# First modulation of a two-layer diffusion backbone: four steps of two K chunks instead of five steps

## The chip, the cores and the metric

One core of a Trainium2 chip runs the whole program. The metric is the device time of one execution in microseconds (us), lower is better. In the profile the engines are PE (TensorE matmul), PEld (TensorE weight load), DVE (VectorE), ACT (ScalarE), POOL (GpSimd) and SP (SyncE, which here issues every DMA; SPq is its queue). L12 stands for line 12 of the kernel.

## The reference, cut to what matters

Two layers (DEPTH 2) of width D = 1024 work on 256 latent tokens `x` and 256 context tokens `ctx`. Each layer is a half-step gated FFN, a mixer (neighbourhood attention in layer 0, a short convolution in layer 1) and another half-step FFN. Only the very start matters here:

```
m  = (silu(c)     @ ada_w[0] + ada_b[0])   # 9 vectors of 1024, latent tokens
mc = (silu(c_ctx) @ ada_w[0] + ada_b[0])   # the same for the context tokens
h  = x   * (1 + m[1])  + m[0]              # first modulation
hc = ctx * (1 + mc[1]) + mc[0]
a, u = split(h @ ffn_w_in[0, 0], 2);  g = silu(a) * u     # first FFN (and the same for hc)
```

All is float32. Products of matrices are made from two reduced-precision parts: every operand is split into `hi` (rounded) and `lo` (the rest), and each product is hi*hi + lo*hi + hi*lo, three matmuls.

## The kernel before

**Tiling.** The K dimension of 1024 is cut into eight chunks of 128 (`KC = 8`). The first FFN keeps its output transposed: one matmul of `f0_mm` (L537 hi*hi, L538 lo*hi, L539 hi*lo) has 128 columns of the weight as the stationary side and all 512 tokens, latent and context, as the moving side, into one PSUM bank of 128x512. Six banks are open at once (`b0`, `b1`), so that a K chunk serves six groups `g` of three matmuls, eighteen matmuls in all; the eight chunks make 144.

**The start in steps.** Before the first FFN can use a K chunk, its modulation has to be there. `start_step(k0, n)` makes it for n chunks beginning at k0: it loads the columns of two modulation vectors from `ada_w` (L478, tiles `ar`), the bias `ada_b` (L481, tile `ab`, once for four chunks) and the columns of x and ctx (L485, tiles `x` and `xc`, for two chunks at a time); it multiplies silu(c) and silu(c_ctx) with the `ada_w` tiles on PE (L490, result `ada`), adds the bias (L495, `rows`), turns x into columns (L500, `xT`), turns the rows into per-partition columns (L522, `mc`; L524 and L525, `mcol`), and calls `mod`. Of these, `mod` reads the transposed x from PSUM twice: ACT makes `hi` (`h0h`, L509, scale and bias as per-partition operands, rounded on writing), then DVE makes the unrounded value (`h`, L513) and `lo` = value minus hi (`h0l`, L515). The steps are (0,1), (1,1), (2,2), (4,2), (6,2): two of one chunk and three of two. A generator yields between the parts, and the loop over `steps` puts them between the groups of `f0_mm` of the step before; the tables `NA` and `NB` say how many parts go ahead of each group.

**Weights.** `w1(p, [u])` loads a pair of weight blocks for panel p and K chunks 2u and 2u+1 (two DMAs of 256 KB, L175, tile `w1r`), and splits them: ACT makes `w1h` in two halves (L178), DVE `w1l` in two halves (L181).

**Order.** PE runs in the order of the program text (`manual_schedule`). The instructions of ACT, DVE and of SP's DMA queue are ordered by a list scheduler at build time: by priority, which is the order of the text, moved ahead by `tc.high_priority(offset=...)`, and by when the scheduler thinks that the inputs are ready; the order is then fixed, and every engine runs its list strictly in order. In the start, `w_early[0]` is 0 (no offset for the weights' split), and `mod` has the offset `W_EARLY` = 40. Tiles come from pools with few buffers: `ar` tiles from two pools of together five free buffers, raw weights from four (`WB`), the PSUM banks of `ada`, `xT` and `mc` from two (`PB["tp"]`).

Of the kernel before, what the change touches and what calls it, by code (L numbers as in the profile page):

```python
# [32 lines left out]
W_EARLY = 40  # L33
# [1 line left out]
LN_EARLY = 60  # L35
LEAD = 5
TAIL = 3
XAT = 1
A_LAG = 2
A_PRE = 2  # L40
NX_AT = 2
# [13 lines left out]
V_EARLY = 70  # L55
W_HI = 2
W_LO = 2
NA = (1, 2, 1, 0, 0, 0)
NB = (2, 2, 1, 0, 0, 0)
E0 = (0,)  # L60
E2 = (0, 5, 7)

# [2 lines left out]
def backbone_kernel(  # L65
# [6 lines left out]
    nc = tc.nc  # L72
    sync = nc.sync
# [7 lines left out]
    hp = phase.__enter__()  # L81

    uid = [0]
    w_early = [0]
# [16 lines left out]
    def tpb(s="tp"):  # L101
        return bank("tp", s)
# [59 lines left out]
    def wunit(srcs, kn, s):  # L162

        raw = wp.tile([P, UN], F32, tag="wr", bufs=WB[0], name=nm(s + "r"))
        ext[1] += 1
        if ext[0] and ext[1] % (5 + ext[0]) in (E0 if ext[0] == 1 else E2):
            hi = hp.tile([P, UN], F32R, tag="whx", bufs=ext[0], name=nm(s + "h"))
            lo = hp.tile([P, UN], F32R, tag="wlx", bufs=ext[0], name=nm(s + "l"))
        else:
            hi = wp.tile([P, UN], F32R, tag="wh", bufs=WB[1], name=nm(s + "h"))  # L170
            lo = wp.tile([P, UN], F32R, tag="wl", bufs=WB[2], name=nm(s + "l"))
        rv, hv, lv = (t[:, :kn * 512].rearrange("p (a b) -> p a b", a=kn) for t in (raw, hi, lo))
        with tc.high_priority(offset=w_early[0]):
            for src, c in srcs:
                sync.dma_start(rv[:, :, c:c + src.shape[2]], src)  # L175
            m = kn * 512
            for a in range(0, m, m // W_HI):
                nc.scalar.activation(hi[:, a:a + m // W_HI], raw[:, a:a + m // W_HI], AF.Copy)  # L178
            for a in range(0, m, m // W_LO):
                b = a + m // W_LO  # L180
                nc.vector.tensor_tensor(out=lo[:, a:b], in0=raw[:, a:b], in1=hi[:, a:b].bitcast(F32), op=ALU.subtract)  # L181
        return hv, lv
# [5 lines left out]
    def wpair(w, u, c0, c1, s):  # L188
        if c1 == c0 + 256:
# [26 lines left out]
                            in1=idv[:, 1, :, 0:2], op=ALU.add)  # L216
# [234 lines left out]
    xt = []  # L451
# [6 lines left out]
    mcol = cp.tile([P, KC, 2, 2], F32, tag="mcol", name="mcol")  # L458
# [4 lines left out]
    def start_tile():  # L463
        nar[0] += 1
        if nar[0] % 5 in (2, 4):
            return hp.tile([P, 2, 512], F32, tag="pt", bufs=4, name=nm("ar")).rearrange("p a b -> p (a b)")
        return hp.tile([P, D], F32, tag="ar", bufs=3, name=nm("ar"))

    def start_step(k0, n):

        ps = tpb("ada")
        m = n * P
        kt = 512 // m
        last = KC // kt - 1
        for a in range(KC // kt):
            w = start_tile().rearrange("p (k m c) -> p k m c", k=kt, m=2)
            for i in range(2):
                sync.dma_start(w[:, :, i], bass.AP(ada_w.tensor, ada_w.offset + a * kt * P * 9 * D + i * D + k0 * P,  # L478
                                                   [[9 * D, P], [P * 9 * D, kt], [1, m]]))
            if a == last and k0 % 4 == 0:  # L480
                sync.dma_start(ab0[k0 // 4][0:64], bass.AP(ada_b.tensor, ada_b.offset + k0 * P, [[D, 2], [0, 32], [1, 512]]))  # L481
            if a == (last if k0 else XAT) and k0 % 2 == 0:
                for t in range(4):
                    src = x[0] if t < 2 else ctxt[0]
                    sync.dma_start(xt[t][k0 // 4][:, k0 % 4 * P:k0 % 4 * P + 256],  # L485
                                   src[(t % 2) * P:(t % 2 + 1) * P, k0 * P:k0 * P + 256])
            for i in range(kt):
                for j in range(2):
                    o = 64 * (i % 2) + 32 * j
                    nc.tensor.matmul(ps[o:o + 32, 0:m], cst[:, a * kt + i, :], w[:, i, j, :],  # L490
                                     start=(a == 0 and i < 2), stop=(a == last and i >= kt - 2))
            if (a + 1) % (n if n == 1 else 2) == 0:
                yield
        rows = sp.tile([P, 256], F32, tag="s2", bufs=S2, name=nm("rows"))
        nc.vector.tensor_tensor(out=rows[:, 0:m], in0=ps[:, 0:m], in1=ab0[k0 // 4][:, k0 % 4 * P:k0 % 4 * P + m], op=ALU.add)  # L495

        def xT(k):
            px = tpb("xT")
            for t in range(4):
                nc.tensor.transpose(px[:, t * P:(t + 1) * P], xt[t][k // 4][:, (k % 4) * P:(k % 4 + 1) * P], ident)  # L500
            return px

        def mod(k, px):
            t = sp.tile([P, 512], F32, tag="s2", bufs=S2, name=nm("h"))
            hi, lo = act(F32R, "h0h"), act(F32R, "h0l")
            with tc.high_priority(offset=W_EARLY):
                for v in range(2):
                    s = slice(v * 256, (v + 1) * 256)
                    nc.scalar.activation(hi[:, s], px[:, s], AF.Identity, bias=mcol[:, k, 0, v:v + 1],  # L509
                                         scale=mcol[:, k, 1, v:v + 1])  # L510
                for v in range(2):
                    s = slice(v * 256, (v + 1) * 256)
                    nc.vector.tensor_scalar(t[:, s], px[:, s], mcol[:, k, 1, v:v + 1], mcol[:, k, 0, v:v + 1],  # L513
                                            op0=ALU.mult, op1=ALU.add)
                nc.vector.tensor_tensor(out=lo, in0=t, in1=hi.bitcast(F32), op=ALU.subtract)  # L515
            hT0.append((hi, lo))

        px = xT(k0)
        yield
        pc = tpb("mc")  # L520
        for i in range(n):
            nc.tensor.matmul(pc[:, 4 * i:4 * i + 4], rows[:, i * P:(i + 1) * P], sel, start=True, stop=True)  # L522
        pv = pc[:, 0:4 * n].rearrange("p (k m v) -> p k m v", k=n, m=2)
        nc.vector.tensor_copy(mcol[:, k0:k0 + n, 0, :], pv[:, :, 0, :])  # L524
        nc.vector.tensor_scalar(mcol[:, k0:k0 + n, 1, :], pv[:, :, 1, :], 1.0, None, op0=ALU.add)  # L525
        mod(k0, px)
        yield
        if n > 1:
            mod(k0 + 1, xT(k0 + 1))
            yield  # L530

    def f0_mm(ps, units, j, z, ks):
        s = slice(z * 256 + j * P, z * 256 + (j + 1) * P)
        for k in ks:
            hi, lo = units[k // UK]
            lh, ll = hi[:, k % UK, s], lo[:, k % UK, s]
            nc.tensor.matmul(ps, lh, hT0[k][0], start=(k == 0), stop=False)  # L537
            nc.tensor.matmul(ps, ll, hT0[k][0], start=False, stop=False)  # L538
            nc.tensor.matmul(ps, lh, hT0[k][1], start=False, stop=(k == KC - 1))  # L539
# [31 lines left out]
    w_early[0] = W_EARLY  # L571
# [315 lines left out]
    steps = [(h + i, qt) for h in range(0, NH, 2) for qt in range(2) for i in range(2)]  # L887
# [10 lines left out]
    for i in range(len(steps) + LAG + V_LAG):  # L898
# [13 lines left out]
        n = int(credit)  # L912
# [10 lines left out]
        j = i - LAG - V_LAG  # L923
# [77 lines left out]
    g, hTs, later = sub_end(sc_w_out[0], lhs_T(yT), KC, 1, 1, 5, 1.0, (1, 6), "wo", order_late(KU))  # L1001
# [56 lines left out]
```

## Time and profile before

| | us |
|---|---|
| median of three runs | 1295.72 |
| the three runs | 1291.27, 1295.72, 1295.99 |
| the profiled execution, as a whole | 1290.21 |
| its span, first to last instruction | 1288.4 |
| PE busy in the span | 1256.5 (98%) |
| DVE busy | 954.7 (74%) |
| ACT busy | 591.0 (46%) |
| instructions | 17192 |

The profile is one execution taken by the hardware profiler. A row of a timeline begins with the start in the span and a duration, then the engine, the line, the operation, output and inputs, and in brackets how long the engine was idle before and what it was waiting for. A row of the grouped view has the shapes, the count, and after the bar the summed busy time in us and the mean in ns. The busy time of a matmul is modelled and reaches over the start of the next one, so the distance between two starts says more than the duration.

### The profile page before, as it was taken

The page shows a single profiled execution, that of the slowest core. Times are in us where ns is not written, and L with a number is a line of the kernel's source. Part 1 is how long each engine was busy: PE and PEld are TensorE (multiplying, and loading weights), DVE is VectorE, ACT ScalarE, POOL GpSimd, SP SyncE. Part 2 cuts the span into 40 slices and gives each one's busy share as a digit, 9 for nine tenths or more (in the row PEclk, how much of TensorE's full clock was granted, in tenths as well). Part 3 has the DMA queues.
Part 4 walks back from the last instruction along what each step waited for, and adds up shares of the span by engine and source line. Part 5 has one row for each costly group of instructions (what it writes and reads, how often), then busy time and mean ns, then how long its engine had stood idle before and what let it go on. Part 6 is the DMA issues. An engine that isn't in the chain of part 4 may idle for free.

```text
span 1288.4 us, 17192 instructions
## 1 busy us (share of the span) xinstructions
PE 1256.5 (98%) x5890; PEld 1005.4 (78%) x5890; DVE 954.7 (74%) x1683; ACT 591.0 (46%) x1148; POOL 40.4 (3%) x69
## 2 busy tenths in 40 slices
PE   7999999999999999988999999999999999999997
PEld 4787778788778877766787787887788877788886
DVE  3599877595658767788997888867878688855545
ACT  2433132412326456677554535645435645655431
POOL 0000000000001111120000000000000000000000
PEclk9999999999999999989999999999999999999999
DMA  9978668484622744464998988677887764676641
GB/s 285 284 238 260 187 187 289 153 299 150 216 66 85 217 90 90 92 149 130 314 333 267 325 315 298 205 220 222 290 298 244 211 218 147 214 213 187 226 158 50
DMA packets 204018, 271.26 MB, mean 211 GB/s; under 512 B 30028, under 2 KB 149300, under 8 KB 203930
## 3 DMA queue, kind: packets, MB, share of 16 engines
q1 hardware_dynamic: 203930, 270.16, 66.9%
q8 instruction: 46, 0.75, 0.2%
q14 instruction: 42, 0.34, 0.1%
HBM read 267.93 MB, written 2.17 MB: 210 GB/s over the span
## 4 chain that ended last, share of the span: by engine, by line
PE 81%; DVE 7%; DMA 6%; ACT 3%; issue 1%; SPq 1%; POOL 0%; DVEq 0%; ACTq 0%
PE w L156 15%; PE w L157 14%; PE w L159 14%; PE f L537 6%; PE f L539 6%; PE f L538 6%; DMA w1r<-in_ffn_w_in_dram 4%; DVE w1l L181 2%; PE wkv L156 2%; PE wkv L159 2%; PE wkv L157 2%; PE wc L156 2%; PE wc L157 2%; PE wc L159 2%; DMA ar<-in_ada_w_dram 1%
## 5 line engine op out<-in xcount | busy, mean ns | idle before, releaser
L178 ACT ACTIVATE w1h<-w1r 128x512 fp32r<-128x512 f32 x352 | 203.1, 626 | 185.7 <-PE w L159 71.4
L181 DVE TENSOR_TENSOR w1l<-w1r,w1h 128x512 fp32r<-128x512 f32 x352 | 227.6, 685 | 66.7 <-ACT w1h L178 63.5
L156 PE MATMUL w<-w1h,hTh 128*128 128x512 f32 x528 | 210.8, 399 | 3.3 <-ACT hTh L105 3.3
L243 DVE SCALAR_TENSOR_TENSOR acc<-ar,cst,acc 128x512 f32<-128x512 f32 x266 | 187.5, 746 | 33.6 <-DMA ar<-in_ada_w_dram 33.3
L157 PE MATMUL w<-w1l,hTh 128*128 128x512 f32 x528 | 207.0, 392 | 0.0
L156 PE MATMUL w<-w2h,gh 128*128 128x512 f32 (+1 forms) x446 | 175.4, 394 | 0.0
L157 PE MATMUL w<-w2l,gh 128*128 128x512 f32 (+1 forms) x446 | 173.4, 389 | 0.0
L178 ACT ACTIVATE w2h<-w2r 128x512 fp32r<-128x512 f32 x176 | 101.5, 624 | 140.9 <-PE w L159 122.2
L159 PE MATMUL w<-w1h,hTl 128*128 128x512 f32 x528 | 163.4, 391 | 0.7 <-DVE hTl L106 0.7
L181 DVE TENSOR_TENSOR w2l<-w2r,w2h 128x512 fp32r<-128x512 f32 x176 | 114.0, 686 | 42.1 <-ACT w2h L178 41.4
L537 PE MATMUL f<-h0h,w1h 128*128 128x512 f32 x352 | 139.3, 396 | 0.0
L539 PE MATMUL f<-h0l,w1h 128*128 128x512 f32 x352 | 137.8, 392 | 0.0
L538 PE MATMUL f<-h0h,w1l 128*128 128x512 f32 x352 | 137.8, 391 | 0.0
L159 PE MATMUL w<-w2h,gl 128*128 128x512 f32 (+1 forms) x446 | 136.3, 387 | 0.0
L156 PEld LDWEIGHTS w<-w1h,hTh 128*128 128x128 f32 x528 | 99.2, 188 | 27.2 <-ACT hTh L105 4.6
L159 PEld LDWEIGHTS w<-w1h,hTl 128*128 128x128 f32 x528 | 98.9, 188 | 23.9 <-DVE hTl L106 1.5
L157 PEld LDWEIGHTS w<-w1l,hTh 128*128 128x128 f32 x528 | 99.2, 188 | 20.3 <-DVE w1l L181 0.3
L156 PEld LDWEIGHTS w<-w2h,gh 128*128 128x128 f32 x446 | 83.7, 188 | 21.8 <-issue 1.7
L159 PEld LDWEIGHTS w<-w2h,gl 128*128 128x128 f32 x446 | 83.3, 188 | 18.8
L157 PEld LDWEIGHTS w<-w2l,gh 128*128 128x128 f32 x446 | 83.7, 188 | 17.4
L537 PEld LDWEIGHTS f<-h0h,w1h 128*128 128x128 f32 x352 | 66.2, 188 | 17.9 <-issue 4.1
L539 PEld LDWEIGHTS f<-h0l,w1h 128*128 128x128 f32 x352 | 66.2, 188 | 14.4
(176 smaller groups left out, 1703.1 us busy)
## 6 DMA issues: line engine op xcount, KB each, us to landing
w1r<-in_ffn_w_in_dram SPq DMA_DIRECT2D x352, 256.0 KB
ar<-in_ada_w_dram SPq DMA_DIRECT2D x128, 512.0 KB
w2r<-in_ffn_w_out_dram SPq DMA_DIRECT2D x88, 512.0 KB
ar<-in_ada_w_dram SPq DMA_DIRECT2D x32, 256.0 KB
wkvr<-in_na_w_qkv_dram SPq DMA_DIRECT2D x32, 256.0 KB
wcr<-in_sc_w_in_dram SPq DMA_DIRECT2D x32, 256.0 KB
wqr<-in_na_w_qkv_dram SPq DMA_DIRECT2D x8, 512.0 KB
bias<-in_na_rpb_dram SPq DMA_DIRECT2D x64, 64.0 KB
```

Source lines behind the costliest of these rows:

```text
L156: nc.tensor.matmul(ps, lh, rh, start=first and i == 0, stop=False)
L157: nc.tensor.matmul(ps, lh, rl, start=False, stop=False)
L159: nc.tensor.matmul(ps, ll, rh, start=False, stop=last and i == n - 1)
L178: nc.scalar.activation(hi[:, a:a + m // W_HI], raw[:, a:a + m // W_HI], AF.Copy)
L181: nc.vector.tensor_tensor(out=lo[:, a:b], in0=raw[:, a:b], in1=hi[:, a:b].bitcast(F32), op=ALU.subtract)
L243: nc.vector.scalar_tensor_tensor(out=a, in0=src, scalar=sc, in1=a, op0=ALU.mult, op1=ALU.add)
L537: nc.tensor.matmul(ps, lh, hT0[k][0], start=(k == 0), stop=False)
L538: nc.tensor.matmul(ps, ll, hT0[k][0], start=False, stop=False)
L539: nc.tensor.matmul(ps, lh, hT0[k][1], start=False, stop=(k == KC - 1))
```

## The change

- The first modulation is made in four steps of two chunks, (0,1), (2,3), (4,5), (6,7). The first step therefore multiplies with 256 columns of each of the two vectors, in four `ar` tiles, where it had 128 columns in two.
- Within a step the order of the DMAs is: two `ar` tiles, `ab` (for k0 = 0 and 4), two `ar` tiles, then x and ctx. Before, `ab` came right ahead of x and ctx, behind all `ar` tiles of its step.
- In the loop, the matmuls of chunks 0 and 1 are now run chunk by chunk in 12 groups of three, and those of the later pairs in six groups of six; the parts of the next step go behind the groups listed in `at`.
- In `mod`, DVE makes the unrounded value from PSUM for each half of the tokens (latent, context), ACT copies it from SBUF to get `hi`, and DVE makes `lo` in two halves.
- The first weight unit is requested inside the first step, between the modulations of chunks 0 and 1, with the offset 40 for its split and none for its DMA.

```diff
-    def start_step(k0, n):
+    def start_step(k0):
         ps = tpb("ada")
-        m = n * P
+        m = 2 * P
         kt = 512 // m
         last = KC // kt - 1
...
-            if a == last and k0 % 4 == 0:
+            if a == 1 and k0 % 4 == 0:
                 sync.dma_start(ab0[k0 // 4][0:64], ...)
-            if a == (last if k0 else XAT) and k0 % 2 == 0:
+            if a == last:
                 for t in range(4):
                     src = x[0] if t < 2 else ctxt[0]
                     sync.dma_start(xt[t][k0 // 4][...], src[...])
...
-            if (a + 1) % (n if n == 1 else 2) == 0:
+            if a % 2:
                 yield
...
+            h = [slice(v * 256, (v + 1) * 256) for v in range(2)]
             with tc.high_priority(offset=W_EARLY):
                 for v in range(2):
-                    s = slice(v * 256, (v + 1) * 256)
-                    nc.scalar.activation(hi[:, s], px[:, s], AF.Identity, bias=mcol[:, k, 0, v:v + 1],
-                                         scale=mcol[:, k, 1, v:v + 1])
+                    nc.vector.tensor_scalar(t[:, h[v]], px[:, h[v]], mcol[:, k, 1, v:v + 1], mcol[:, k, 0, v:v + 1],
+                                            op0=ALU.mult, op1=ALU.add)
+                    nc.scalar.activation(hi[:, h[v]], t[:, h[v]], AF.Copy)
                 for v in range(2):
-                    s = slice(v * 256, (v + 1) * 256)
-                    nc.vector.tensor_scalar(t[:, s], px[:, s], mcol[:, k, 1, v:v + 1], mcol[:, k, 0, v:v + 1],
-                                            op0=ALU.mult, op1=ALU.add)
-                nc.vector.tensor_tensor(out=lo, in0=t, in1=hi.bitcast(F32), op=ALU.subtract)
+                    nc.vector.tensor_tensor(out=lo[:, h[v]], in0=t[:, h[v]], in1=hi[:, h[v]].bitcast(F32), op=ALU.subtract)
...
         mod(k0, px)
+        if k0 == 0:
+            w_early[0] = W_EARLY
+            u0.extend(w1(0, [0]))
+            w_early[0] = 0
         yield
-        if n > 1:
-            mod(k0 + 1, xT(k0 + 1))
-            yield
+        mod(k0 + 1, xT(k0 + 1))
+        yield
...
-    steps = ((0, 1), (1, 1), (2, 2), (4, 2), (6, 2))
-    run(start_step(*steps[0]))
-    for q, (k0, n) in enumerate(steps):
-        nxt = start_step(*steps[q + 1]) if q < 4 else iter(())
-        for g in range(6):
-            if g == 0 and k0 % 2 == 0:
-                u0 += w1(0, [k0 // 2])
-            for _ in range((NA if q == 0 else NB)[g]):
-                next(nxt, 0)
-            if g == 0 and k0 % 2 == 0:
-                u1 += w1(1, [k0 // 2])
-            p, j, z = g // 4, g // 2 % 2, g % 2
-            f0_mm((b0[j], b1)[p][z], (u0, u1)[p], j, z, range(k0, k0 + n))
+    run(start_step(0))
+    for k0 in range(0, KC, 2):
+        if k0:
+            u0 += w1(0, [k0 // 2])
+        u1 += w1(1, [k0 // 2])
+        nxt = start_step(k0 + 2) if k0 + 2 < KC else iter(())
+        if k0 == 0:
+            o = [(g, (k,)) for k in (0, 1) for g in range(6)]
+            at = (4, 6, 8, 9, 10)
+        else:
+            o = [(g, (k0, k0 + 1)) for g in range(6)]
+            at = (0, 1, 2, 3, 4)
+        for n, (g, ks) in enumerate(o):
+            f0_mm((b0 + [b1])[g // 2][g % 2], (u0, u1)[g // 4], g // 2 % 2, g % 2, ks)
+            if n in at:
+                next(nxt, 0)
         run(nxt)
```

The rest of the kernel, from the panel after the 144 matmuls on, is the same text.

More of the change, by code (lines that the diff above doesn't have):

```diff
@@ L37 @@
 TAIL = 3
-XAT = 1
 A_LAG = 2
@@ L57 @@
 W_LO = 2
-NA = (1, 2, 1, 0, 0, 0)
-NB = (2, 2, 1, 0, 0, 0)
 E0 = (0,)
@@ L83, in backbone_kernel @@
     uid = [0]
-    w_early = [0]
+    w_early = [0, 0]
     ext = [1, 0]
@@ L172, in wunit @@
         rv, hv, lv = (t[:, :kn * 512].rearrange("p (a b) -> p a b", a=kn) for t in (raw, hi, lo))
-        with tc.high_priority(offset=w_early[0]):
+        with tc.high_priority(offset=min(w_early)):
             for src, c in srcs:
                 sync.dma_start(rv[:, :, c:c + src.shape[2]], src)
+        with tc.high_priority(offset=w_early[0]):
             m = kn * 512
@@ L479, in start_step @@
                                                    [[9 * D, P], [P * 9 * D, kt], [1, m]]))
-            if a == last and k0 % 4 == 0:
+            if a == 1 and k0 % 4 == 0:
                 sync.dma_start(ab0[k0 // 4][0:64], bass.AP(ada_b.tensor, ada_b.offset + k0 * P, [[D, 2], [0, 32], [1, 512]]))
-            if a == (last if k0 else XAT) and k0 % 2 == 0:
+            if a == last:
                 for t in range(4):
                     src = x[0] if t < 2 else ctxt[0]
-                    sync.dma_start(xt[t][k0 // 4][:, k0 % 4 * P:k0 % 4 * P + 256],
-                                   src[(t % 2) * P:(t % 2 + 1) * P, k0 * P:k0 * P + 256])
+                    sync.dma_start(xt[t][k0 // 4][:, k0 % 4 * P:k0 % 4 * P + m],
+                                   src[(t % 2) * P:(t % 2 + 1) * P, k0 * P:k0 * P + m])
             for i in range(kt):
@@ L520, in start_step @@
         pc = tpb("mc")
-        for i in range(n):
+        for i in range(2):
             nc.tensor.matmul(pc[:, 4 * i:4 * i + 4], rows[:, i * P:(i + 1) * P], sel, start=True, stop=True)
-        pv = pc[:, 0:4 * n].rearrange("p (k m v) -> p k m v", k=n, m=2)
-        nc.vector.tensor_copy(mcol[:, k0:k0 + n, 0, :], pv[:, :, 0, :])
-        nc.vector.tensor_scalar(mcol[:, k0:k0 + n, 1, :], pv[:, :, 1, :], 1.0, None, op0=ALU.add)
+        pv = pc[:, 0:8].rearrange("p (k m v) -> p k m v", k=2, m=2)
+        nc.vector.tensor_copy(mcol[:, k0:k0 + 2, 0, :], pv[:, :, 0, :])
+        nc.vector.tensor_scalar(mcol[:, k0:k0 + 2, 1, :], pv[:, :, 1, :], 1.0, None, op0=ALU.add)
         mod(k0, px)
+        if k0 == 0:
+            w_early[0] = W_EARLY
+            u0.extend(w1(0, [0]))
+            w_early[0] = 0
         yield
-        if n > 1:
-            mod(k0 + 1, xT(k0 + 1))
-            yield
+        mod(k0 + 1, xT(k0 + 1))
+        yield
     def f0_mm(ps, units, j, z, ks):
@@ L570, in backbone_kernel @@
     sync.dma_start(rope, rope_tab.rearrange("(t p) a b -> p t a b", p=P))
-    w_early[0] = W_EARLY
+    w_early[:] = [W_EARLY, W_EARLY]
     set_background(stream([(0, 2, 0), (0, 2, 1)], [(0, 3, 0), (0, 3, 1)], [(0, 4, 0), (0, 4, 1)],
```

## The prediction

> **What bounds the kernel now.** I read busy time by stretch first, to see where PE is not full, then what PE waited for in the start.
>
> ```profile
> span 1288.4 us, 17192 instructions
> 0.00:10.00 10.00, 3.65 (x33) 1.70 (x33) 1.30 (x5) 1.67 (x3) 0.78 (x9) 1.00 0.71 200
> 10.00:20.00 10.00, 7.35 (x47) 4.41 (x48) 4.90 (x11) 3.32 (x6) 0.00 (x0) 1.00 0.99 306
> 20.00:30.00 10.00, 10.00 (x75) 7.53 (x74) 4.19 (x12) 3.73 (x8) 0.00 (x0) 1.00 1.05 332
> 30.00:40.00 10.00, 8.31 (x60) 4.81 (x59) 3.61 (x10) 1.50 (x4) 0.00 (x0) 1.00 0.93 273
> 66.00:400.00 334.00, 334.00 (x1478) 268.43 (x1477) 248.87 (x403) 95.44 (x167) 1.49 (x4) 1.00 0.63 200
> ...
> PE ada L490 <- DMA ar<-in_ada_w_dram: 3.8, 4, 1.9
> PE xT L500 <- DMA x<-in_x_dram: 3.7, 2, 2.3
> ```
>
> The columns of the first part are the stretch, its length, busy time of PE, PEld, DVE, ACT, POOL, the granted clock, the DMA share and GB/s. PE is short by 6.35 us in the first ten, 2.65 in the second and 1.69 from 30 to 40, some 10.7 us in all, and waits there for DMAs alone; DMA is near its limit from 10 on. From 66 to 400 PE is busy 334.00 of 334. So the start is bound by transfers and by the way to the first matmuls, and what the change shifts there goes one for one into the end, because PE has nothing to wait for behind it for hundreds of us. The question is when PE is through with the 144 matmuls.
>
> ```profile
> 45.75 1.93 PE L490 MATMUL ada<-ar,cst 128*32 128x256 f32 x32
> 47.61 0.50 PE L537 MATMUL f<-h0h,w1h 128*128 128x512 f32 x1
> ...
> 49.11 0.38 PE L500 MATMUL xT<-ident,x 128*128 128x128 f32 x2
> ...
> 49.55 0.51 PE L522 MATMUL mc<-sel,rows 128*128 128x4 f32 x4
> 49.91 0.48 PE L537 MATMUL f<-h0h,w1h 128*128 128x512 f32 x1
> ...
> 57.37 0.39 PE L537 MATMUL f<-h0h,w1h 128*128 128x512 f32 x1
> ...
> 65.56 0.39 PE L537 MATMUL f<-h0h,w1h 128*128 128x512 f32 x1
> ```
>
> The last 36 of the 144 start at 57.37 and the first of the next panel at 65.56: 0.2275 us each. By starts, an `ada` step is 1.86, one `xT` 0.44, one `mc` 0.36. From the first of the 144 on, the new order holds 144 x 0.2275 = 32.8, three ada 5.6, six xT 2.6 and three mc 1.1: 42.1 us without a wait. Before, this ended at 65.56, as if it had begun at 65.56 - 42.1 = 23.5 and never waited. That 23.5 is what the change has to beat.
>
> **When the first matmul can start.**
>
> ```profile
> 3.63 0.67 SPq L481 DMA_DIRECT2D ab<-in_ada_b_dram  x1
> ...
> 7.60 0.62 PEld L490 LDWEIGHTS ada<-ar,cst 128*32 128x32 f32 x14 [0.58 <-DMA ar<-in_ada_w_dram]
> ...
> 11.54 0.52 PEld L500 LDWEIGHTS xT<-ident,xc 128*128 128x128 f32 x2 [0.16 <-DMA xc<-in_ctx_dram]
> ...
> 4.00:6.00 2.00, 1.14 (x13) 0.68 (x16) 0.00 (x0) 0.00 (x0) 0.00 (x0) 1.00 0.99 282
> 18.00:20.00 2.00, 2.00 (x21) 1.46 (x21) 0.59 (x2) 0.00 (x0) 0.00 (x0) 1.00 1.10 353
> ```
>
> Before, the first step's 1 MiB of `ar` was in at 7.60, and `ab` (128 KiB) and x (512 KiB) at 11.54: 3.94 us for 0.655 MB, which at 282 GB/s is 2.3. The bias costs 1.6 us over its bytes. Now the step has 2 MiB ahead of x. Pieces of one row are 1 KiB instead of 512 bytes; bounds for the rate are 282 GB/s (512-byte pieces here) and 353 (mostly 1 KiB, later). A MiB is then 3.7 to 3.0 us. At the fast end, to which the new pieces are nearer, x lands at 11.54 - 0.7 (first MiB faster) + 3.0 = 13.8; at the slow end at 15.2; if part of the bias's 1.6 hides behind the second MiB, at 12.8. Then, in a row, the last transposes 0.6, `mc` at twice its 0.36 on a slow PE, 0.7, and the modulation below, 2.0 with `mcol` and hand-overs: first matmul at **17.1**, bounds 15.9 to 18.5. The first weight unit comes 512 KiB behind x, 1.5 us, and its split on ACT and DVE fits or adds half a us to the second matmul; I take 0.5.
>
> ```profile
> 14.86 1.08 PE L490 MATMUL ada<-ar,cst 128*32 128x128 f32 x14 [0.79 <-DMA ar<-in_ada_w_dram]
> 15.87 0.80 PE L537 MATMUL f<-h0h,w1h 128*128 128x512 f32 x1
> 16.46 0.63 PE L538 MATMUL f<-h0h,w1l 128*128 128x512 f32 x1
> 16.89 0.63 PE L539 MATMUL f<-h0l,w1h 128*128 128x512 f32 x1
> ...
> 19.46 0.48 PE L537 MATMUL f<-h0h,w1h 128*128 128x512 f32 x1
> ```
>
> The first matmuls are also slow: 16.46 to 16.89 is 0.43, against 0.23 later. PE works nearly without a break from 14.86 on; at 16.89 it is still slow and by 19.46 (0.48 long instead of 0.80) no longer, so slowness lasts 2.6 to 4.6 us of steady work, though the granted clock reads 1.00 throughout. In the new order PE is mostly idle ahead of 17.1, so I take 3.6 us at about half speed from there: 1.7 lost (bounds 0 and 2.2). The Trainium skill, TensorE: Matmul & The Clock Gate, Part 1, says that the array runs at half rate until some 3.4 us of sustained activity. By that the loss is the same 1.7; if PE were warm already the sum would gain 1.7 more, and the row's clock of 1.00 does not settle it, the distances do, on the page's side.
>
> Equivalent start: 17.1 + 0.5 + 1.7 = 19.3, against 23.5. **4.2 us ahead.**
>
> **hi and lo from SBUF.**
>
> ```profile
> L509 ACT ACTIVATE h0h<-xT,mcol 128x256 fp32r<-128x256 f32 x16 | 8.2, 562 | 34.4 <-DVE mcol L525 34.4
> L513 DVE TENSOR_SCALAR h<-xT,mcol 128x256 f32<-128x256 f32 x16 | 8.0, 540 | 5.8 <-ACT h0h L509 5.8
> L515 DVE TENSOR_TENSOR h0l<-h,h0h 128x512 fp32r<-128x512 f32 x8 | 5.5, 688 | 0.1
> L105 ACT ACTIVATE oT<-osum 128x256 fp32r<-128x256 f32 x8 | 3.3, 410 | 1.6 <-DVE osum L851 1.6
> L106 DVE TENSOR_TENSOR oT<-osum,oT 128x256 fp32r<-128x256 f32 x8 | 4.4, 553 | 1.6 <-ACT oT L105 1.4
> ```
>
> Before: ACT twice 0.5 (hi ready after 1.0), DVE waits for it, twice 0.5, then 0.69: lo after some 2.7. Now: DVE 0.54, 0.5, ACT's second half 0.41 behind: hi after 1.5 to 1.6; lo's halves 0.42 to 0.55: after 2.1. DVE carries eight instructions more, 16 x 0.55 - 5.5 = 3.3 us at most over 48 us in which it was mostly idle. DVE's wait for ACT (5.8 us) ended nowhere on PE, so removing it gives nothing by itself; hi comes 0.5 later.
>
> That matters through the new places of the parts. Before, two groups at most stood ahead of `xT` and `mc`, and 24 matmuls (5.5 us) behind the last `xT` hid the modulation. Now `mc` comes behind group 9 of 12 (three matmuls each) or 3 of 6 (six each). For 0 to 2: behind `mc` stand 0.68 + 0.44 + 0.68 = 1.8 us of PE work; both modulations take, on DVE, 0.3 + 1.05 + 0.85 (with the wait for hi) + 1.05, then ACT 0.5: hi of chunk 3 some 3.9 us behind `mc`, wanted at 1.8 + 0.68 = 2.5. **Wait 1.3.** For 2 to 4 and 4 to 6: PE has 1.37 + 0.44 + 1.37 + 0.68 = 3.9: it just fits. What DVE does between decides:
>
> ```profile
> 39.82 1.00 DVE L513 TENSOR_SCALAR h<-xT,mcol 128x256 f32<-128x256 f32 x2 [1.15 <-ACT h0h L509]
> 40.73 0.69 DVE L181 TENSOR_TENSOR w1l<-w1r,w1h 128x512 fp32r<-128x512 f32 x1
> ...
> 41.94 0.69 DVE L181 TENSOR_TENSOR w1l<-w1r,w1h 128x512 fp32r<-128x512 f32 x1
> ```
>
> The scheduler fills DVE's gaps with `w1l` at 0.6 each, and the order is then fixed. I take 0.4 for each of the two transitions (between nothing and two `w1l`, 1.2).
>
> **ada_b ahead, and the transfers behind.**
>
> ```profile
> 28.09 0.56 SPq L481 DMA_DIRECT2D ab<-in_ada_b_dram  x1
> ...
> 33.23 0.37 SPq L478 DMA_DIRECT2D ar<-in_ada_w_dram  x1
> 36.60 0.37 SPq L175 DMA_DIRECT2D w1r<-in_ffn_w_in_dram  x1
> ...
> 33.78 0.50 PE L537 MATMUL f<-h0h,w1h 128*128 128x512 f32 x1
> ...
> 36.63 0.42 DVE L495 TENSOR_TENSOR rows<-ada,ab 128x256 f32<-128x256 f32 x1 [3.86 <-DMA ab<-in_ada_b_dram]
> 36.87 0.50 PE L500 MATMUL xT<-ident,x 128*128 128x128 f32 x2 [1.42 <-DMA x<-in_x_dram]
> 36.00:38.00 2.00, 1.10 (x6) 0.69 (x6) 0.42 (x1) 0.00 (x0) 0.00 (x0) 1.00 0.45 137
> ```
>
> The second `ab`, issued at 28.09, lands at 36.6, and the eighth DMA behind it, `w1r`, is issued only then: SP stands still for 3.4 us and the DMA rate falls to 137 GB/s. The bytes stay: x of step 4 is behind `ab` before and after. What moves is that the second MiB of `ada_w` for step 4 is now behind `ab` too. Before, it was in by 33.7 (the first group behind it starts at 33.78). Now 512 KiB of weights more stand ahead of it (1.5), and `ab` with 1.6 and 0.4 for its bytes; less 0.7 of the faster first MiB and about 1.0 for the standstill of SP at the first `ab`: 35.5. PE wants it at 19.3 + 11.3 (eight-chunk quarter: 8.2 + 1.86 + 0.88 + 0.36) + 1.3 + 0.93 + 2 x 1.37 = 35.6. No wait, but transfers are a ceiling here: whoever comes earlier waits till 35.5. The Trainium skill, DMA: Bandwidth & Descriptors, "Why a DMA increments its semaphore by 16 and not by 1", says that a DMA is spread over as many engines as divide its slowest dimensions; `ab`'s source has two rows there, so two engines would carry 64 KiB each, an estimate of 2.3 us at that page's rate per engine, wherever in the queue it stands. By it the gain falls by 0.3; were `ab` spread evenly (0.4 us), it would grow by 1.6. The 1.6 us above its bytes stands nearer the rule.
>
> **The sum.** 4.2 - 1.3 - 0 - 0.8 = 2.1 us earlier. Against the profiled execution's 1290.21 (span 1288.4 and 1.8 around it) that is 1288.1. That execution lies 5.5 below the median of the runs shown and 1.1 below the lowest. The four times (1290.21, 1291.27, 1295.72, 1295.99) have a mean of 1293.3, so I say **1291.2**.
>
> **Rivals.**
> 1. The modulation is hidden and the transfers come on time: the 1.3 and 0.8 vanish and PE is through 4.2 earlier, with a warm PE or an early x (12.8) up to 7. For it: DVE is 42% busy from 20 to 30. Against it: the ceiling at 35.5, behind which 27.2 us of PE work remain (0.93 + 5.5 + 1.24 + 11.3 + 8.2), ends at 62.7, 2.9 earlier; more needs faster transfers than any row shows. About 1289.
> 2. Slower: `w1l` in DVE's fixed order between the parts of `mod`. Three in each of the three transitions add 1.8 each: 3.1 + 1.9 + 1.9 = 6.9 lost against 4.2 won, 2.7 slower, **1296**. It decides from about 1.5 `w1l` per transition on. For it: two stood between in the rows above, and `mc` comes later now. Against it: `mod` still has the offset of 40, and the weights' split none.
> 3. The change gives nothing: the larger first step delays x as much as the saved step brings (x at 15.2 and the slow PE at its bound), 1293.3.
>
> **How the numbers follow.** Forecast (0.5 to 4 earlier) 0.50; rival 1 0.18, a third of it beyond 6.5; rival 2 0.20; rival 3 0.12. Half a per cent is 6.5 us, about what a measurement can tell from no change; only the far ends of rivals 1 and 2 and the unsteady runs (4.7 us between lowest and highest) reach it: faster 0.09, same 0.84, slower 0.07. The range takes the lowest time less the 6 us of rival 1 and the highest with the 2.7 of rival 2: 1285 to 1298. The forecast's own is 1288 to 1295.
>
> **What would show it.** First L537 at 17.1 and its distances of 0.43 for some eight matmuls; the first L537 of the next panel at 63.5; PE waiting for `h0h` or `h0l` of chunks 2 and 3, about 1.3; L509's successor at 0.41 and no wait of DVE for ACT ahead of L513. Wrong if x of step 0 lands past 15.2, if the waits for `h0h` and `h0l` sum above 4, or if the difference of the spans is not that of the starts of that L537.

## The result and the profile after

The changed kernel takes 1302.05 us (median of six runs) against 1293.62 (six runs of the kernel before): 1.0064 times as long, 95% interval 1.0047 to 1.008. It is slower by 8.4 us, outside the range forecast, and on the other side. Its profiled execution took 1303.63 us.

The stretches of the span of the kernel after, with the columns as before:

```profile
span 1301.9 us, 17127 instructions
30.00:40.00 10.00, 7.20 (x38) 4.69 (x40) 5.95 (x14) 3.01 (x7) 0.00 (x0) 0.90 0.98 279
50.00:60.00 10.00, 8.36 (x50) 4.62 (x50) 3.95 (x10) 3.12 (x7) 0.00 (x0) 0.83 0.78 253
75.50:400.00 324.50, 324.50 (x1432) 260.77 (x1432) 241.09 (x389) 91.70 (x157) 0.00 (x0) 1.00 0.64 202
```

What PE waited for in its first 76 us (line, tile, us in total, times, longest):

```profile
PE ada L488 <- DMA ar<-in_ada_w_dram: 5.4, 3, 3.4
PE f L537 <- DVE w1l L179: 4.4, 3, 1.6
PE f L536 <- ACT h0h L509: 1.2, 1, 1.2
```

From 75.5 to 400 PE has no gap, as before from 66 to 400. The loss lies ahead of that. New are the holes from 30 to 40 and 50 to 60, where PE waits for `w1l` (the low half of the next weight unit, split by DVE) and the granted clock falls to 0.90 and 0.83. PE's own timeline, from the last pieces of the first step to the next panel (L536 is now hi*hi, L537 lo*hi):

```profile
12.05 3.11 PE L488 MATMUL ada<-ar,cst 128*32 128x256 f32 x16 [3.38 <-DMA ar<-in_ada_w_dram]
15.09 0.69 PE L498 MATMUL xT<-ident,x 128*128 128x128 f32 x2
...
19.55 0.80 PE L536 MATMUL f<-h0h,w1h 128*128 128x512 f32 x1 [1.19 <-ACT h0h L509]
...
24.01 0.51 PE L536 MATMUL f<-h0h,w1h 128*128 128x512 f32 x1
...
34.13 0.49 PE L536 MATMUL f<-h0h,w1h 128*128 128x512 f32 x1
36.26 0.50 PE L537 MATMUL f<-h0h,w1l 128*128 128x512 f32 x1 [1.63 <-DVE w1l L179]
...
36.83 0.40 PE L536 MATMUL f<-h0h,w1h 128*128 128x512 f32 x1
38.40 0.80 PE L537 MATMUL f<-h0h,w1l 128*128 128x512 f32 x1 [1.17 <-DVE w1l L179]
...
39.55 1.92 PE L488 MATMUL ada<-ar,cst 128*32 128x256 f32 x16
41.40 0.50 PE L536 MATMUL f<-h0h,w1h 128*128 128x512 f32 x1
...
51.80 0.50 PE L536 MATMUL f<-h0h,w1h 128*128 128x512 f32 x1
53.95 0.50 PE L537 MATMUL f<-h0h,w1l 128*128 128x512 f32 x1 [1.64 <-DVE w1l L179]
...
75.55 0.39 PE L536 MATMUL f<-h0h,w1h 128*128 128x512 f32 x1
```

The row at 75.55 is the first matmul of the next panel, which began at 65.56 before: 10.0 us later. The prediction's own sum says where. It was 17.1 (first matmul) + 0.5 + 1.7 (slow start) + 42.1 (PE's work) + 2.1 (waits) = 63.5. Measured: 19.55 + 2.4 (nine matmuls took 24.01 - 19.55 = 4.46 instead of 9 x 0.2275 = 2.05) + 42.1 + 11.5 = 75.55. So the first matmul is 2.45 late, the slow start is as forecast (2.4 for 2.2), and the waits are 9.4 dearer. By the starts of two neighbours less the usual 0.23, the three stops for `w1l` cost 1.9 + 1.3 + 1.9 = 5.1. The ada half-step at 39.55 is 1.85 long (1.00 where the clock is 1.00); with the matmuls around it and behind the third stop the slow clock costs some 3. Some 3.3 remain, in small steps in all four rounds: mostly matmuls next to an `ada`, `xT` or `mc`, which come 0.31 to 0.37 apart instead of 0.23 and which the sum had at nothing.

Why `w1l` is late stands in the timelines of ACT and DVE of the same kernel. ACT first:

```profile
28.36 0.63 ACT L176 ACTIVATE w1h<-w1r 128x512 fp32r<-128x512 f32 x1 [6.65 <-DMA w1r<-in_ffn_w_in_dram]
33.21 0.87 ACT L509 ACTIVATE h0h<-h 128x256 fp32r<-128x256 f32 x2 [4.21 <-DVE h L507]
```

And DVE:

```profile
32.36 0.16 DVE L520 COPY mcol<-mc 128x4 f32<-128x4 f32 x1 [2.60 <-PE mc L518]
...
32.63 1.52 DVE L507 TENSOR_SCALAR h<-xT,mcol 128x256 f32<-128x256 f32 x3
34.06 0.75 DVE L511 TENSOR_TENSOR h0l<-h,h0h 128x256 fp32r<-128x256 f32 x2
...
35.52 0.68 DVE L179 TENSOR_TENSOR w1l<-w1r,w1h 128x512 fp32r<-128x512 f32 x1
```

ACT stands idle for 4.21 us and DVE for 2.60, both at the head of lists whose next entry belongs to the late modulation; the weights' split, without an offset, is listed behind it. That unit's data had landed by 28.36, when ACT split its first half, so the second half and both `w1l` waited for their place in the lists and not for a transfer. DVE makes the first `w1l` at 35.52, and PE goes on at 36.26. Idle engines here are the sign of a late input ahead of an urgent instruction.

The first matmul is late, in good part because of the bias. SP's queue of the same kernel:

```profile
3.50 0.67 SPq L479 DMA_DIRECT2D ab<-in_ada_b_dram  x1
4.21 2.09 SPq L476 DMA_DIRECT2D ar<-in_ada_w_dram  x4
...
7.56 4.32 SPq L483 DMA_DIRECT2D xc<-in_ctx_dram  x2
12.02 2.40 SPq L172 DMA_DIRECT2D w1r<-in_ffn_w_in_dram  x4
```

Issuing two DMAs takes SP 4.32 us there instead of some 1.0: the second is the eighth behind `ab`. The weights leave only at 12.02. The last `ada_w` pieces were issued right behind `ab`, by 6.30 and so ahead of that stop, but PE can use them only in the group that begins at 12.05 and makes room for the transposes at 15.09. So what holds PE up is that they land late, not that SP stands still.

Beyond 75.55, the spans of the two profiles drift apart further, by 13.5 in all, and the medians by only 8.4. A second profile of the kernel before (the last experiment) accounts for it.

### The profile page after: what moved, and what is told of

It reads as the page before. It is cut to its first block, busy times and chain, and to the rows that moved or that the text cites. A ratio compares the mean times of both kernels' runs of the same rounds, so it can differ in the third digit from the quotient of the medians.

```text
span 1301.9 us, 17127 instructions
## 1 busy us (share of the span) xinstructions
PE 1263.8 (97%) x5858; PEld 1006.5 (77%) x5858; DVE 954.3 (73%) x1688; ACT 588.8 (45%) x1148; POOL 42.5 (3%) x69
## 4 chain that ended last, share of the span: by engine, by line
PE 77%; DMA 9%; DVE 8%; ACT 3%; issue 2%; SPq 1%; POOL 0%; DVEq 0%; ACTq 0%; POOLq 0%
PE w L153 13%; PE w L154 13%; PE w L156 13%; PE f L536 6%; PE f L537 6%; PE f L538 6%; DMA w1r<-in_ffn_w_in_dram 4%; DMA ar<-in_ada_w_dram 3%; DVE w1l L179 2%; PE wkv L153 2%; PE wkv L156 2%; PE wkv L154 2%; PE wc L153 2%; PE wc L154 2%; PE wc L156 2%
## 5 line engine op out<-in xcount | busy, mean ns | idle before, releaser
L537 PE MATMUL f<-h0h,w1l 128*128 128x512 f32 x352 | 139.5, 396 | 4.4 <-DVE w1l L179 4.4
L536 PE MATMUL f<-h0h,w1h 128*128 128x512 f32 x352 | 141.3, 401 | 1.2 <-ACT h0h L509 1.2
L536 PEld LDWEIGHTS f<-h0h,w1h 128*128 128x128 f32 x352 | 66.9, 190 | 21.9 <-issue 5.8
L537 PEld LDWEIGHTS f<-h0h,w1l 128*128 128x128 f32 x352 | 67.1, 191 | 19.5 <-DVE w1l L179 5.8
```

## The experiments

"First" is the start of the first matmul of f, "panel" that of the first one of the next panel (65.56 before, 75.55 after), both from one profile; the ratio is the time against the kernel before, run beside it.

| run | kernel and edit | median us | ratio (95%) | first | panel |
|---|---|---|---|---|---|
| e1 | after, next weight unit ahead of mod | 1297.34 | 1.0026 (1.0011 to 1.0040) | 18.72 | 71.12 |
| e2 | after, parts placed earlier | 1296.30 | 1.0022 (1.0005 to 1.0038) | 18.05 | 68.89 |
| e3 | after, hi from PSUM again | 1300.83 | 1.0054 (1.0035 to 1.0073) | 17.31 | 75.33 |
| e4 | after, bias in two DMAs | 1297.28 | 1.0041 (1.0020 to 1.0062) | 16.41 | 72.24 |
| e5 | before, bias in two DMAs | 1289.55 | 0.9976 (0.9963 to 0.9988) | 15.46 | 65.77 |
| e6 | after, e1 + e2 + e4 | 1292.85 | 1.0005 (0.9993 to 1.0017) | 16.41 | 65.33 |
| e7 | after, bias last in its step again | 1301.45 | 1.0069 (1.0050 to 1.0088) | 19.57 | 75.00 |
| e8 | before, hi and lo from SBUF | 1291.54 | 0.9996 (0.9978 to 1.0013) | 15.41 | 65.36 |
| e9 | after, PE kept busy ahead of the first | 1297.00 | 1.0023 (1.0007 to 1.0038) | 20.52 | 72.59 |
| e10 | e6 + e9 | 1289.86 | 0.9974 (0.9958 to 0.9989) | 16.42 | 64.36 |
| e11 | e5, PE kept busy | 1291.36 | 0.9986 (0.9969 to 1.0003) | 15.50 | 66.36 |
| e12 | before, a second profile | 1294.53 | one run | 16.17 | 65.60 |

The theory: the order on ACT and DVE (split behind the modulation) and the late places of the parts made the stops, and the bias's one DMA held up the start. The rivals: the longer chain to hi through SBUF; the place of the bias; the slow start of PE. "First" itself moves from profile to profile: the group of `ada` that begins at 12.05 in the kernel after begins at 11.22, 11.06 and 11.08 in e1 to e3, with the same DMAs ahead of it, so a shift of 1.0 us in "first" needs no edit.

**e1, the next weight unit ahead of the modulation.**

```diff
+        if k0:
+            w_early[0] = W_EARLY
+            u0.extend(w1(0, [k0 // 2]))
+            w_early[0] = 0
         pc = tpb("mc")
...
-        if k0:
-            u0 += w1(0, [k0 // 2])
```

> The changed kernel, with the unit of panel 0 for the next pair of chunks requested, and its split into hi and lo put with the same priority as the modulation, ahead of that modulation in the text; the DMAs keep their places. Theory 'order' (in the fixed lists of ACT and DVE the split of the next weights stands behind the late modulation, and PE waits for w1l): PE's 4.4 us of waiting for w1l go to under 1, the slow matmuls behind them go too, the modulation comes 1 us later; the first hi*hi matmul of the next panel moves from 75.6 to 69-71 us, the time falls by 4 to 6. Theory 'chain' (hi and lo from SBUF take too long): that start stays at 75 or grows, since the modulation only gets later. Theory 'transfers' (the doubled first step and the bias among the tiles): unchanged within 1 us.

PE's waits in the same stretch:

```profile
PE ada L488 <- DMA ar<-in_ada_w_dram: 4.6, 3, 2.6
PE f L540 <- ACT h0h L509: 3.1, 4, 1.2
```

The waits for `w1l` are gone and the panel comes 4.4 earlier, 0.8 of it already at the first matmul, ahead of which the edit changes nothing. In their place the waits for `h0h` grow from 1.2 to 3.1: now the modulation is what is late. Order is part of the cause, not all of it.

**e2, the parts of the next step placed earlier.**

```diff
-            at = (4, 6, 8, 9, 10)
+            at = {4: 1, 6: 1, 7: 1, 8: 1, 9: 1}
...
-            at = (0, 1, 2, 3, 4)
+            at = {0: 1, 1: 2, 2: 2}
...
-            if n in at:
+            for _ in range(at.get(n, 0)):
                 next(nxt, 0)
```

> The changed kernel, with the parts of the next step put further ahead: for the later pairs one behind group 0, two behind group 1, two behind group 2 (of 6), and for the first pair behind groups 4, 6, 7, 8, 9. Theory 'order': modulation and split both come about two groups (2.7 us) earlier against PE, the waits for w1l of the later pairs go to about 0, that of the first pair to about 1: next panel from 75.6 to 69-71. Theory 'chain': the same direction, since the modulation has more cover; it differs from 'order' in e1 alone. Theory 'transfers': PE waits for ar and x instead, next panel at 74-76.

PE's waits:

```profile
PE f L537 <- DVE w1l L179: 1.7, 2, 0.9
PE f L536 <- ACT h0h L509: 1.7, 1, 1.7
PE xT L498 <- DVE mcol L521: 1.2, 3, 0.4
```

The panel comes 6.7 earlier with DVE's and ACT's priorities as they were; 1.5 of that lie ahead of the first matmul, in a step that the edit does not touch. `w1l` is waited for only from chunks 0 to 1 into 2 and 3; behind the later pairs no such wait is left. With more matmuls between `mc` and its use, the same order does little harm: the place decides how much the order costs.

**e3, hi and lo as before the change**, ACT reading PSUM.

```diff
-                    nc.scalar.activation(hi[:, h[v]], t[:, h[v]], AF.Copy)
+                    nc.scalar.activation(hi[:, s], px[:, s], AF.Identity, bias=..., scale=...)
...
-                    nc.vector.tensor_tensor(out=lo[:, h[v]], in0=t[:, h[v]], in1=hi[:, h[v]].bitcast(F32), op=ALU.subtract)
+                nc.vector.tensor_tensor(out=lo, in0=t, in1=hi.bitcast(F32), op=ALU.subtract)
```

> The changed kernel, with hi made by ACT from PSUM and lo in one piece as before the change. Theory 'chain': the waits go, next panel at 66 or earlier. Theory 'order': the lists of ACT and DVE still hold modulation and split in one another's way; 0 to 2 loses some 4 us as now, 2 to 4 less (about 0.5 instead of 1.9): next panel at 72-73, time 2 to 3 less than the changed kernel's. 'Transfers': unchanged.

PE's wait for lo:

```profile
PE f L540 <- DVE h0l L513: 3.7, 4, 1.6
```

The first matmul comes 2.2 earlier, of which 1.0 is the earlier landing of `ada_w` and not the edit, and the panel 0.2, not at the 72 to 73 that the theory of order gave. What hi gains, lo loses: 3.7 us of waits for `h0l`. The longer chain to hi is not where the 10 us went.

**e4, the bias in two DMAs**, each from one row of `ada_b` into 32 partitions.

```diff
-                sync.dma_start(ab0[k0 // 4][0:64], bass.AP(ada_b.tensor, ..., [[D, 2], [0, 32], [1, 512]]))
+                for j in range(2):
+                    sync.dma_start(ab0[k0 // 4][32 * j:32 * j + 32],
+                                   bass.AP(ada_b.tensor, ada_b.offset + j * D + k0 * P, [[0, 32], [1, 512]]))
```

> The changed kernel, with the bias in two DMAs of 32 partitions each instead of one of 64 whose source has an outer dimension of 2; same bytes. If the bias is slow because it runs on two DMA engines, it lands about 2 us earlier, the SP queue no longer stands still behind x (4.3 us now), the last ar of step 0 lands 2 us earlier and the first matmul of the FFN starts at about 17.5 instead of 19.55; if it is slow because one row is read 32 times, nothing moves. What of it reaches the next panel: 'order' 0 to 2 us (the waits for w1l are set by the lists, not by transfers), 'transfers' the full 2 or more.

The same two DMAs in SP's queue:

```profile
7.48 0.99 SPq L485 DMA_DIRECT2D xc<-in_ctx_dram  x2
```

And the first matmul in PE's timeline:

```profile
16.41 0.69 PE L538 MATMUL f<-h0h,w1h 128*128 128x512 f32 x1 [1.65 <-ACT h0h L511]
```

The same bytes, read from the same rows as often, and SP no longer stops: 0.99 instead of 4.32. The first matmul comes 3.1 earlier and the panel 3.3; against e1 and e2, which have the bias in one DMA too, the first matmul comes 2.3 and 1.6 earlier. So what is slow is how the one DMA is cut, not the repeated reading. The Trainium skill, DMA: Bandwidth & Descriptors, "Why a DMA increments its semaphore by 16 and not by 1", gives a transfer as many engines as divide its slowest dimensions; two rows make two engines, 32 partitions make sixteen. The trace agrees, though it doesn't show the engines one by one: the bias's 64 packets of 2 KiB run from 6.80 to 10.59 in the kernel after, at most 4 at a time, and from 5.87 to 6.92 in e4, up to 13 at a time.

**e5, the same diff in the kernel before.**

> The kernel before the change with one edit: the bias of chunks 0 to 3 and 4 to 7 (128 KiB each) comes in two DMAs of 32 partitions instead of one of 64, so that the source's outer dimension is 32 and not 2. Order, places and arithmetic stay. Theory (the bias's one DMA holds up what is behind it, and SP with it): in the changed kernel the same edit brought the first L536 forward by 3.1 us (19.55 to 16.41) and the next panel's start by 3.3. In the kernel before, the first group stands behind the same landing (x of step 0 came behind the first bias at 11.54 against 2.3 us of bytes), so its first matmul comes 1 to 2 us earlier (15.87 to about 14.4), the 3.86 us wait of `rows` for the second bias and the 1.42 us wait of the transposes for x at 36.9 shrink or go, and the next panel starts 1.5 to 3.5 earlier, at 62 to 64 (65.56): time 1.5 to 3.5 us below before, ratio 0.997 to 0.999. Rival (the bias's cost hides behind other transfers there, since PE has 24 matmuls ahead of each step): next panel at 65 to 66, ratio 1.000.

PE's waits up to the panel:

```profile
PE ada L492 <- DMA ar<-in_ada_w_dram: 6.5, 8, 1.8
PE xT L502 <- DMA xc<-in_ctx_dram: 0.6, 1, 0.6
```

The first matmul comes 0.4 earlier and the panel 0.2 later, at 65.77 and not at 62 to 64: the waits for x turned into waits for `ar`, as the rival said, since transfers bound that start. Yet the time falls by 3.1 us, with an interval that leaves 1.0 out. The panel's start does not explain this; where the 3 us come from stays open.

**e6, the edits of e1, e2 and e4 together.**

> The changed kernel with three edits of the runs so far together: the first weight unit of the next pair of chunks is asked for ahead of the modulation (e1), the five parts of the next step are placed earlier (e2), and the bias comes in two DMAs (e4). Alone they brought the next panel's start from 75.55 to 71.12, 68.89 and 72.24. If order, places and bias are the whole of the loss and their gains add where they don't overlap (places and order work on the same waits, so I count the larger of the two, 6.7, plus 3.2 for the bias, plus what was left of w1l in e2, up to 1.7): next panel at 64 to 66, that is as in the kernel before (65.56) or 1.5 earlier, ratio 0.998 to 1.001. Rival (four steps of two chunks can't be covered by the PE work that stands between, whatever the order): waits swap names and the next panel stays above 67, ratio 1.001 to 1.003.

PE's waits, and then the panel's first matmul in its timeline:

```profile
PE f L542 <- ACT h0h L511: 2.5, 2, 1.7
PE xT L500 <- DVE mcol L527: 1.2, 3, 0.4
```

```profile
65.33 0.39 PE L542 MATMUL f<-h0h,w1h 128*128 128x512 f32 x1
```

All 10 us are back, and no wait for `w1l` is left: order, places and the cut of the bias together make up for the whole loss. The first step accounts for 3.1 of it, what follows the first matmul for 7.1. That does not make four steps better than five: 0.2 earlier, and no difference in time.

**e7, the bias last in its step again.**

```diff
-            if a == 1 and k0 % 4 == 0:
+            if a == last and k0 % 4 == 0:
```

> The changed kernel with one part undone: the bias is asked for with the last piece of ada_w again, not behind the second. If its place in the queue is what cost the start (it stands ahead of the last pieces of ada_w and held them up to about 15), the last ada_w comes in some 2 us earlier but rows then waits for the bias instead, in the same order of landing: first matmul within 1 us of 19.55, next panel within 1.5 of 75.55. If the place were the loss itself, both come 3 us earlier, as with the bias in two DMAs (16.41 and 72.24).

First matmul within 0.02 of 19.55 and the panel 0.55 earlier. The place in the queue costs nothing either way; wherever the bias stands, x or `ada_w` behind it waits.

**e8, hi and lo from SBUF alone, in the kernel before**: the lines of `mod` from the diff of the change.

> The kernel before the change with one part of it alone: hi and lo of the first modulation are taken from the modulated row in SBUF (DVE first, then ACT), lo in two halves. Theory (it neither gains nor loses where 24 matmuls cover the modulation; in the changed kernel, undoing it moved the next panel by 0.2): next panel within 1 us of 65.56, ratio 0.999 to 1.001. Rival (the eight more DVE instructions and hi half a us later cost on PE as well): next panel 1.5 to 3 later, ratio 1.001 to 1.002.

The panel comes 0.2 earlier and the ratio holds 1.0. With 24 matmuls of cover the edit is free.

**e9, PE kept busy ahead of the first matmul**: 25 transposes of `ident` whose results are overwritten.

```diff
+    def warm(n):
+        for _ in range(n):
+            nc.tensor.transpose(b0[0][0][:, 0:P], ident, ident)
...
+            if k0 == 0 and a < last:
+                warm(4)
...
-        mod(k0 + 1, xT(k0 + 1))
+        if k0 == 0:
+            warm(3)
+        px = xT(k0 + 1)
+        if k0 == 0:
+            warm(10)
+        mod(k0 + 1, px)
```

> The changed kernel with 25 transposes of `ident` (128x128, into the first bank of f, whose first matmul starts it afresh) put into PE's gaps ahead of the first matmul: four behind each of the first three pieces of ada_w, three behind `mc`, ten behind the transposes of chunk 1. They compute nothing that is used. Theory (the first matmuls are 0.43 apart because PE was idle ahead of them): they run 0.23 apart from the start or after at most three, the slow stretch of 9 matmuls shrinks by 1.5 to 2 us, the first matmul stays within 0.6 of 19.55, and the next panel starts 1 to 2 us earlier than 75.55 (the scheduler also moves one split of the first unit on ACT, worth up to 0.5 at the first matmul). The slow clock behind the w1l waits at 36 to 40 and 54 to 58 stays. Rival (the slow start has another cause, cold data or instruction fetch): 9 to 10 matmuls 0.43 apart as before.

PE's timeline around the first matmuls:

```profile
18.53 2.34 PE L469 MATMUL f<-ident 128*128 128x128 f32 x10
20.52 0.78 PE L547 MATMUL f<-h0h,w1h 128*128 128x512 f32 x1
21.09 0.53 PE L548 MATMUL f<-h0h,w1l 128*128 128x512 f32 x1
21.46 0.40 PE L549 MATMUL f<-h0l,w1h 128*128 128x512 f32 x1
```

And the stretches of the first two stops:

```profile
34.00:36.00 2.00, 0.81 (x3) 0.48 (x3) 2.00 (x6) 0.88 (x3) 0.00 (x0) 1.00 0.93 263
36.00:38.00 2.00, 1.43 (x15) 0.71 (x18) 1.28 (x3) 0.00 (x0) 0.00 (x0) 1.00 0.68 205
```

Two slow matmuls instead of nine: the slow start does come from PE's idleness ahead of it. The transposes themselves ran at half clock (0.50 granted from 18.5 to 20.5) and overran the first matmul by 1.0, more than the 0.6 allowed. Two things were not expected: the second stop shrank (1.17 to 0.57, ACT's list is not quite the same), and no slow clock followed there. So 3.0 are gained instead of 1 to 2: 0.95 at the start, the rest there. The run is not a clean test of the start alone.

**e10, e6 and the transposes of e9** (both diffs).

> The changed kernel with the three edits (unit first, parts early, bias in two DMAs) and the same 25 transposes. With the three edits alone the first matmul came at 16.41, 8 matmuls were 0.43 apart at a recorded clock of 0.59 and 0.55, and the next panel began at 65.33. ACT's and DVE's orders stay but for one pair on DVE. Theory of the clock: 1.2 to 1.7 us earlier, next panel at 63.6 to 64.2, time 1.5 us under that of the three edits, ratio to before 0.998 to 1.0. Rival (what starts earlier waits longer for mcol and h0h, or for transfers): next panel at 65 or later, ratio as with the three edits, 1.0005.

PE's timeline, the first matmul of f and the panel's:

```profile
16.42 0.50 PE L553 MATMUL f<-h0h,w1h 128*128 128x512 f32 x1 [0.57 <-ACT h0h L517]
...
64.36 0.39 PE L553 MATMUL f<-h0h,w1h 128*128 128x512 f32 x1
```

The first matmul comes when it did, none is slow, and the panel begins 1.0 earlier than in e6 (1.2 to 1.7 expected; waits of 0.4 for `h0l` took a part). The ratio of 0.9974 means 3.4 us below the kernel before, and by the two ratios some 12 below the changed one, so this version beats both; of those 3.4 the panel shows 1.2.

**e11, e5 with PE kept busy**: 28 such transposes, six behind each of the first two pieces of ada_w and sixteen behind `mc`.

> The kernel before with the bias in two DMAs and with 28 transposes of `ident` in PE's gaps of the first step. With the bias alone the first matmul came at 15.46 and the next panel at 65.77, while PE waited 6.5 us for ar: the transfers were its bound. Theory (transfers bound the kernel before, so a faster PE at the start is given back as waits for ar): next panel within 0.7 of 65.77, time within 1.5 of the one with the bias alone, ratio 0.9965 to 0.9985. Rival (PE's slow start is on the path): next panel at 64 to 64.5.

The scheduler put three `w1l` ahead of the first lo, where e5 has one, and PE stood 2.4 us for `h0l` behind its second matmul and then ran at a clock of 0.50 for some 6 us. The panel still comes only 0.6 later than in e5: PE's waits for `ar` fell from 6.5 to 2.7. That shows the slack that transfers give this start, by another way than meant; since DVE's order changed with the edit, it is no clean test of the clock.

**e12, the kernel before again.**

> The kernel before, unchanged, profiled a second time, to see how far one profile's milestones can be trusted: the first matmul and the next panel's start within 0.5 us of 15.87 and 65.56 if the start is the same in every execution, and the span then differs (1288.4 there) by what happens later. If instead transfers land differently from run to run, the next panel's start moves by a us or more.

One stretch of the first profile of the kernel before:

```profile
800.00:810.00 10.00, 7.84 (x37) 5.92 (x37) 7.44 (x14) 7.86 (x20) 1.07 (x2) 1.00 0.55 172
```

The same stretch in this second profile:

```profile
800.00:810.00 10.00, 7.96 (x28) 6.06 (x27) 6.75 (x13) 7.05 (x16) 1.07 (x2) 0.83 0.64 218
```

And in the kernel after, 10 us later:

```profile
810.00:820.00 10.00, 7.91 (x29) 6.02 (x28) 7.10 (x13) 6.91 (x16) 1.07 (x2) 0.83 0.61 200
```

The panel's start differs by 0.04 between the two profiles of the same kernel, the spans by 4.4 (1288.4 and 1292.8). PE is idle for some 2 us there in all three; in two of them a slower clock follows (0.83 over 10 us, 1.7 lost), in the first none does. Over 600 to 1080 PE is busy for 475.27 and 472.93 us in the two, another 2.3. So in the kernel before the panel's start repeats from run to run, though its first matmul moved by 0.3, and the later part does not; the profile on which the forecast rested was a lucky execution. The last section shows why the clock fell in one and not in the other. Against the second one the changed kernel's span is 9.1 longer, near the 10.0 of the panel.

## Why the prediction was wrong

**The step that failed is the cover of the modulation**, "it just fits. What DVE does between decides", with 1.3 and twice 0.4. It counted what DVE might put between the parts of the modulation, and took the modulation as what PE would wait for. The runs show the reverse: the modulation held up the split of the next unit, which stood behind it in the fixed lists of ACT and DVE. A step that just fits has no room for anything that must follow it on the same engine before PE can go on; each transition needs the modulation and one `w1l`. Instead of 2.1 the waits and what followed cost 11.5: 5.1 of stops, some 3 of slow clock behind them, 3.3 of small steps. The small steps belong to PE's work, 42.1 in the sum, which did not have them. e1 takes the stops for `w1l` away by order, e2 most of them by place.

**Slow clock behind stops** was no term of the sum at all; it was counted for the start only. Its size is in part chance: e9 has the same first stop of 1.6 us, a second one of 0.57 and no slow clock behind them.

**The first matmul**, 17.1 with bounds to 18.5, came at 19.55. PE was through with the first step's `ada` at 15.09, where the working had the inputs in at 13.8 (upper bound 15.2). It took the bias's 1.6 us over its bytes from the kernel before as what the bias costs. e4 prices the bias at 3.1 against this profile, which is the dear end of the runs: against e2 it is 1.6, near what the working had, so part of the miss is this execution's transfers. The other 1.15 lie between the last `ada` and the matmul, mostly because ACT split a weight (18.05 to 19.18) between the two halves of hi; the sum had that split at 0.5, behind the first matmul.

**The slow start** (1.7, with 0.5 for the split) was right in size, 2.4, and e9 shows its cause. That the size fits is in part luck: there are 7 slow matmuls at the start of e2 and e4 and 9 here.

**The bias behind, "no wait"**: right, e7 moves the panel by 0.55. **hi and lo from SBUF**, nothing by itself: right, e8 and e3 both move the panel by 0.2, though in e3 this is a sum of shifts that cancel.

**The rivals.** The second came nearest: slower, by `w1l` in DVE's fixed order. But it had `w1l` delaying the modulation and priced the loss at 2.7; its argument against itself, that the modulation has the offset and the split has none, was the cause of what happened. What was not asked is what stands behind the modulation in the list.

**The signs named** worked. The start of the next panel, 75.55 for 63.5, showed the miss at once. Its difference of 10.0 is near that of the spans against the second profile of the kernel before (9.1) and not against the one that the forecast used (13.5), so this sign of being wrong came true as well. The waits for `h0h` and `h0l`, 1.2 against a bound of 4, showed nothing, since the wait was for `w1l`.

**Turning the panel's start into time**: 10.0 there gave 8.4 in the medians. Over e1 to e11 the shift in time lies between 4.0 below and 0.9 above that of the panel, mostly some 2 below; so a difference of up to some 4 us cannot be traced to the start here.

## What to carry to other kernels

When a part of the work is moved later on an engine that runs a fixed list, ask what stands behind it in that list and who waits for that; an engine idle at the head of its list while another waits for an entry further down is the sign of it. Price a stop of PE with the slow matmuls that follow, not by its length alone. A small DMA with a short outer dimension can hold up everything behind it and the queue that issues it; cut it by partitions, which cost nothing here.

## What the runs showed of the hardware

The clock fell to 0.50 behind stops much shorter than expected: no stop ahead of the drop at 37.91 in the kernel after is longer than 1.9 us. The Trainium skill, TensorE: Matmul & The Clock Gate, Part 1, has the array go cold after at least one idle window of some 3.4 us; by this drop less than that is enough when matmuls are sparse. A share of busy time over a stretch cut by hand doesn't settle it: in e9 the clock stayed at 1.00 with 2.24 of four us busy (34 to 38), in e1 it fell with 2.52 of four busy (32 to 36).

That page calls its window free-running, and the traces show such a window. In all fourteen of them every recorded stretch of the granted clock, but the last, is a whole number of 3.41 us, from 1 to 366 of them, so the edges can be read from each trace. Cut along the edges, the kernel after:

```profile
34.49:37.91 3.42, 1.10 (x4) 0.49 (x3) 3.42 (x8) 1.76 (x5) 0.00 (x0) 1.00 0.82 244
37.91:41.32 3.41, 2.92 (x18) 1.10 (x18) 0.43 (x1) 0.00 (x0) 0.00 (x0) 0.50 0.93 274
```

The kernel before around its stop at 800 us, first profile:

```profile
800.71:804.13 3.42, 1.67 (x7) 1.42 (x8) 1.82 (x4) 3.42 (x10) 0.00 (x0) 1.00 0.84 273
804.13:807.54 3.41, 3.41 (x16) 2.76 (x16) 2.89 (x6) 2.44 (x5) 0.84 (x2) 1.00 0.02 6
```

And the same stop in its second profile (e12):

```profile
802.24:805.66 3.42, 1.38 (x6) 0.86 (x5) 1.73 (x3) 3.42 (x11) 0.00 (x0) 1.00 1.03 343
805.66:809.07 3.41, 3.41 (x9) 2.65 (x8) 3.31 (x7) 3.10 (x6) 0.27 (x1) 0.50 0.11 36
```

The clock falls in the window behind one with little work in it. Of some 5,170 such windows at full clock in the fourteen traces, every one with PE busy for less than 1.65 us was followed by a slow one, and none with more than 2.06; between these, both occur. A stop of some 2 us can therefore cost a slow window or not, by where it falls between two edges: that is the 1.7 us that the first profile of the kernel before gained there over its second. The windows of e9 (1.95 busy, 31.63 to 35.04) and e1 (1.92, 33.25 to 36.66) both lie in the band between, and what decides there stays open; the busy time is modelled, and that alone may make the band.

Also, the recorded clock reads 1.00 in the first slow stretch of both kernels (0.43 between matmuls from 19.55 on, and from 16.46 before). The traces' lists of clock stretches begin only at 24.25 in the kernel after and 19.06 before, where the slow matmuls end; a 1.00 ahead of that is no record, and the distances are the safer sign.
